# A causal convolution whose projections recompute the three tokens before each tile, in place of stored history columns

## The chip, the core and the metric

The kernel runs on one core of a Trainium2 chip. The metric is device time in microseconds for one execution, the median of three runs. One more execution was taken with the hardware profiler, and all rows below come from it.

## The reference, cut to what matters

One layer of a streaming encoder over 1024 tokens of 1024 features, in float32: a mixer (gated DeltaNet heads beside an RG-LRU), cross-attention into 256 memory tokens, a product-key expert layer (PEER) and a final RMSNorm. The part that the change touches is the mixer's input projection and the short convolution behind it:

```python
def causal_dwconv(x, w, b=None):
    s = x.shape[1]
    xp = jnp.pad(x, ((0, 0), (CONV_W - 1, 0), (0, 0)))
    y = sum(xp[:, j:j + s] * w[j] for j in range(CONV_W))
    return y if b is None else y + b
...
    proj = h @ w_in
    qkv, z, a_in, b_in, xr, gate = jnp.split(proj, offs, axis=-1)
    qkv = jax.nn.silu(causal_dwconv(qkv, conv_qkv_w))
    ...
    xr = causal_dwconv(xr, lru_conv_w, lru_conv_b)
```

`CONV_W` is 4, so each output token needs the projected columns of its own token and of the three before it. `h` is the RMS-normed input.

## The kernel before

The sequence is worked through in four passes of T = 256 tokens. A pass (`heads`) norms its 256 tokens, transposes them into `hT` (128 features on the partitions, 8 groups of features, 256 tokens), and then projects: `proj_T` loads one weight tile of 512 KB into one of three buffers `w`, and runs eight matmuls that add up 128 output channels x 256 tokens in a PSUM bank `pj`. A float32 matmul stands in the trace as two instructions of TensorE. Sixteen of these projections per pass feed a convolution: tiles 4 to 11 and 0 to 3 are q, k and v of the DeltaNet, tiles 12 to 15 are the LRU input, and four more (16 to 19, the LRU gate) and `wz` feed none. Pass 0 (tokens before `EARLY` = 256) runs its projections as three fp32r products of high and low parts (`Pair`, `mm3`) in place of float32.

`conv` (line 428) works on a buffer `cbuf` of 259 columns, of which there are two. VectorE copies the three columns that the pass before left in `hist` into columns 0 to 2 (line 431). ScalarE copies the 256 projected columns behind them (line 432). VectorE copies the last three back into `hist` for the next pass (line 433). ScalarE writes the newest tap into the output (line 434), and VectorE adds the three older taps from shifted windows of `cbuf` (line 436).

The passes form a chain: `delta` runs the DeltaNet recurrence of a pass in many small matmuls, and starts the next pass's `heads` from within. Beside it runs the stream `attended` (cross-attention, then PEER queries and top-16 searches, `UNITS` of 128 or 256 tokens). PEER's experts are computed in two ways. Tokens 256 to 767 go through a dense product over all experts (`dense`, with one-hot gate tables built by `gates` before it), TensorE's work of the second half. The other 512 tokens are gathered: each of 1024 steps reads 128 rows by an indirect DMA into `rb` (issued by GpSimd) and runs one VectorE instruction of 128x1024 on them. These steps are strewn over the whole kernel.

The order of all this is decided while the program is written. Each engine has a model clock (`Engine`): VectorE is charged 68 ns plus 1.04 ns per element, TensorE 1.67 ns per column of a float32 matmul. `together` always takes a stream whose time has come on TensorE's model clock, and `Paced.tick` puts in a gather step each 2.8 us (later 3.5 us) of TensorE's model time, if VectorE's model clock is less than `SLACK` = 8 us ahead of TensorE's:

```python
            while self.ns > self.pace and (not self.real or dve.at < self.at + SLACK and not late_row()):
                self.ns -= self.pace
                step()
```

In `dense` the steps that are left are spread evenly. Each engine executes its own queue in order.

Of the kernel before, what the change touches and what calls it, by code (L numbers as in the profile page):

```python
# [8 lines left out]
F = mybir.dt.float32  # L9
# [4 lines left out]
AF = mybir.ActivationFunctionType  # L14
# [3 lines left out]
D = 1024  # L18
S = 1024
T = 256  # L20
# [22 lines left out]
EARLY = T  # L43
# [6 lines left out]
def block_kernel(ctx: ExitStack, tc: tile.TileContext, a):  # L50
# [209 lines left out]
    def norm(X, nb, Y, junk):  # L260

        ss = small.tile([128, nb], F, name="n_ss")
        for b in range(nb):
            act.activation(junk, X[b], AF.Square, accum_out=ss[:, b:b + 1])
        dve.tensor_scalar(ss, ss, 1.0 / D, EPS, op0=OP.mult, op1=OP.add)
        rstd = rsqrt(ss, nb, "n_")
        for b in range(nb):
            act.activation(Y[b], X[b], AF.Copy, scale=rstd[:, b:b + 1])
        return rstd
# [15 lines left out]
    def low(i):  # L285

        return early[:, 2 * i:2 * i + 2, :].rearrange("p s (c t) -> p (s c) t", c=D // T)

    def transposed(hT, Y, nb, wcol):

        for c in range(8):
            if c:
                yield 0
            pt = bank("tp", 2)
            for b in range(nb):
                pe.transpose(pt[:, b * 128:(b + 1) * 128], Y[b][:, c * 128:(c + 1) * 128], identf)
            hi = hT.hi if isinstance(hT, Pair) else hT
            act.activation(hi[:, c, :], pt[:, :nb * 128], AF.Copy, scale=wcol[:, c:c + 1])
            if hi is not hT:
                dve.scalar_tensor_tensor(hT.lo[:, c, :], pt[:, :nb * 128], wcol[:, c:c + 1],  # L300
                                         hi[:, c, :].bitcast(F), op0=OP.mult, op1=OP.subtract)
# [122 lines left out]
    def heads(fp, P, prev, qkv):  # L424

        t0, ready = P.t0, P.ready

        def conv(ps, ti, w, out, bias=0.0):

            buf = fp.tile([128, T + 3], F, name="cbuf", bufs=CB)  # L430
            dve.tensor_copy(buf[:, 0:3], hist[:, ti, :])
            act.copy(buf[:, 3:3 + T], ps[:, :T])
            dve.tensor_copy(hist[:, ti, :], buf[:, T:T + 3])
            act.activation(out, ps[:, :T], AF.Identity, scale=w[:, 3:4], bias=bias)
            for j in range(3):
                dve.scalar_tensor_tensor(out, buf[:, j:j + T], w[:, j:j + 1], out, op0=OP.mult, op1=OP.add)

        def tmp():
            return fp.tile([128, T], F, name="cy", bufs=CB)

        while prev and "y" not in prev.ready:
            yield None
        pe.pace = PACES[t0 // T]
        hT = fp.tile([128, 8, T], F, name="hT", bufs=1)
        if prev:
            X = blocks_of(qkv[:, 4:12, :])
            norm(X, NB, X, hT[:, 0:D // T, :].rearrange("p c t -> p (c t)"))
            yield list(X)
        if t0 < EARLY:
            hT = Pair(hT, low(0), tmp)  # L450
        yield from transposed(hT, blocks_of(qkv[:, 4:12, :]), NB, wmixc)


        ps = bank("pj", 2)
        for c in range(8):
            if t0 < EARLY:
                mm3(ps[:8, :T], (wabh[:, c, :], wabl[:, c, :]), (hT.hi[:, c, :], hT.lo[:, c, :]), c == 0, c == 7)
            else:
                pe.matmul(ps[:8, :T], wab[:, c, :], hT[:, c, :], start=c == 0, stop=c == 7)
        abT = fp.tile([128, T], F, name="cth", bufs=1)[:8, :]  # L460
        act.copy(abT, ps[:8, :T])
        pt = bank("tp", 2)
        for b in range(NB):
            pe.transpose(pt[:, b * 8:(b + 1) * 8], abT[:, b * 128:(b + 1) * 128], identf[:8, :8])
        ab = small.tile([128, NB, 8], F, name="ab")
        act.copy(ab, pt[:, :NB * 8])
        if t0 == 0:
            constants()
        xg = small.tile([128, NB, 4], F, name="xg")
        dve.tensor_add(xg, ab[:, :, 0:4], dtb[:, None, :].to_broadcast([128, NB, 4]))  # L470
        spg = softplus(xg.rearrange("p a b -> p (a b)"), NB * 4, "spg").rearrange("p (a b) -> p a b", b=4)
        g = small.tile([128, NB, 4], F, name="g")
        dve.scalar_tensor_tensor(g, spg, -1.0, ealog[:, None, :].to_broadcast([128, NB, 4]),
                                 op0=OP.mult, op1=OP.mult)
        beta = small.tile([128, NB, 4], F, name="beta")
        act.activation(beta, ab[:, :, 4:8], AF.Tanh, scale=0.5)
        dve.tensor_scalar(beta, beta, 1.0, 0.5, op0=OP.add, op1=OP.mult)


        for j in (4, 5, 6, 7, 8, 9, 10, 11, 0, 1, 2, 3):  # L480
            while j == 0 and prev and not prev.finished():
                yield None
            ps = yield from proj_T("wA", j, hT, T)
            y = fp.tile([128, T], F, name="cy", bufs=CB)
            conv(ps, j, hcw[:, j, :], y)
            th = fp.tile([128, T], F, name="cth", bufs=1)
            act.activation(th, y, AF.Tanh)
            dve.scalar_tensor_tensor(qkv[:, j, :], th, 1.0, y, op0=OP.add, op1=OP.mult)

        zs = fp.tile([128, NB, 4, 128], F, name="zs", bufs=1)  # L490
        yl = fp.tile([128, 4, T], F, name="yl", bufs=1)
        P.g, P.beta, P.zs, P.yl = g, beta, zs, yl

        def side():

            for j in range(4):
                ps = yield from proj("wz", j, hT, NB)
                th = fp.tile([128, T], F, name="cth", bufs=1).rearrange("p (b m) -> p b m", b=NB)
                act.activation(th, ps, AF.Tanh, scale=0.5)
                dve.scalar_tensor_tensor(zs[:, :, j, :], th, 1.0, ps, op0=OP.add, op1=OP.mult)  # L500

            ready.add("z")


            for j in range(4):
                ps = yield from proj_T("wA", 12 + j, hT, T)
                xf = fp.tile([128, T], F, name="lxf", bufs=1)
                conv(ps, 12 + j, lconvw[:, j, :], xf, bias=lpar[:, 0, j:j + 1])
                pg = yield from proj_T("wA", 16 + j, hT, T)
                yield L_CONV  # L510
                ge = fp.tile([128, T], F, name="lge", bufs=1)
                act.activation(ge, pg[:, :T], AF.Gelu_apprx_tanh)
                pr = bank("pj")[:, :T]
                pe.matmul(pr, wga[:, j, :], xf, start=True, stop=True)
                px = bank("pj")[:, :T]
                pe.matmul(px, wgx[:, j, :], xf, start=True, stop=True)
                yield 0
                tx = fp.tile([128, T], F, name="ltx", bufs=1)
                act.activation(tx, px, AF.Tanh, scale=0.5, bias=hba[:, 1, j:j + 1])
                dve.scalar_tensor_tensor(tx, tx, 1.0, xf, op0=OP.add, op1=OP.mult)  # L520
                tr = fp.tile([128, T], F, name="ltr", bufs=1)
                act.activation(tr, pr, AF.Tanh, scale=0.5, bias=hba[:, 0, j:j + 1])


                rc = fp.tile([128, T], F, name="lrc", bufs=1)
                act.activation(rc, tr, AF.Exp, scale=nsp4[:, j:j + 1], bias=nsp4[:, j:j + 1])
                act.activation(tr, tr, AF.Tanh, scale=sp2[:, j:j + 1], bias=sp2[:, j:j + 1])
                act.activation(rc, rc, AF.Copy, scale=0.5, bias=0.5)
                nw = xf
                dve.scalar_tensor_tensor(nw, tr, 1.0, rc, op0=OP.add, op1=OP.mult)  # L530
                dve.scalar_tensor_tensor(rc, nw, 2.0, rc, op0=OP.subtract, op1=OP.mult)
                act.activation(tr, tr, AF.Sqrt)
                dve.tensor_mul(tr, tr, rc)
                dve.scalar_tensor_tensor(tx, tr, -1.0, tx, op0=OP.mult, op1=OP.mult)
                act.activation(rc, rc, AF.Copy, scale=-2.0, bias=-1.0)
                dve.tensor_tensor_scan(yl[:, j, :], rc, tx, lstate[:, j:j + 1], op0=OP.mult, op1=OP.add)
                dve.tensor_copy(lstate[:, j:j + 1], yl[:, j, T - 1:T])
                dve.tensor_mul(yl[:, j, :], yl[:, j, :], ge)
            ready.add("y")

        yield Stream(side(), RANK[2], SHARE[2])
# [724 lines left out]
    act.copy(wabh, wab)  # L1266
    dve.tensor_sub(wabl, wab, wabh.bitcast(F))
    norm_x(fp, qkv)
    hist = fc.tile([128, 16, 3], F, name="hist")
    dve.memset(hist, 0.0)  # L1270
    lstate = fc.tile([128, 4], F, name="lstate")
    dve.memset(lstate, 0.0)

# [119 lines left out]
```

## Time and profile before

| | us |
|---|---|
| median of three runs | 3198.26 |
| lowest and highest of them | 3195.79, 3198.62 |
| the profiled execution | 3195.01 |
| its span, first to last instruction | 3193.2 |

The span is what the rows below divide up; 1.8 us lie around it. Mean granted TensorE clock 0.971 of full speed. Over the span TensorE is busy 93% (its matmul ends are modelled and overlap, so this overstates it), VectorE 83%, ScalarE 40%, GpSimd 43%.

### The profile page before, as it was taken

The page shows a single profiled execution, that of the slowest core. Times are in us where ns is not written, and L with a number is a line of the kernel's source. Part 1 is how long each engine was busy: PE and PEld are TensorE (multiplying, and loading weights), DVE is VectorE, ACT ScalarE, POOL GpSimd, SP SyncE. Part 2 cuts the span into 40 slices and gives each one's busy share as a digit, 9 for nine tenths or more (in the row PEclk, how much of TensorE's full clock was granted, in tenths as well). Part 3 has the DMA queues.
Part 4 walks back from the last instruction along what each step waited for, and adds up shares of the span by engine and source line. Part 5 has one row for each costly group of instructions (what it writes and reads, how often), then busy time and mean ns, then how long its engine had stood idle before and what let it go on. Part 6 is the DMA issues. An engine that isn't in the chain of part 4 may idle for free.

```text
span 3193.2 us, 46214 instructions
## 1 busy us (share of the span) xinstructions
PE 2960.5 (93%) x16212; PEld 2535.3 (79%) x16212; DVE 2655.3 (83%) x5871; ACT 1278.3 (40%) x2630; POOL 1361.6 (43%) x1046
## 2 busy tenths in 40 slices
PE   6899899899999898888767999999999999999998
PEld 6889888888888788777656877777888878878886
DVE  7652577897786987998997999888889898889898
ACT  6844264256324531666476323222322222222222
POOL 0000023345332443343423665656565566666563
PEclk9999999999999999998878999999999999999999
DMA  5244768988787678898979899999999999999995
GB/s 175 93 146 146 233 243 315 324 303 308 270 288 272 239 278 314 292 323 285 308 242 318 323 341 337 346 348 343 359 355 351 352 335 339 350 345 353 351 341 212
DMA packets 321544, 941.63 MB, mean 295 GB/s; under 512 B 28912, under 2 KB 108832, under 8 KB 319264
## 3 DMA queue, kind: packets, MB, share of 16 engines
q0 software_dynamic: 148048, 538.04, 47.3%
q1 hardware_dynamic: 107216, 367.08, 31.3%
q10 hardware_dynamic: 66048, 33.56, 3.7%
q8 instruction: 128, 2.10, 0.3%
q14 instruction: 104, 0.85, 0.1%
HBM read 894.53 MB, written 44.04 MB: 294 GB/s over the span
## 4 chain that ended last, share of the span: by engine, by line
PE 33%; DVE 23%; issue 18%; POOL 10%; DMA 9%; ACT 6%; POOLq 0%; SPq 0%; DVEq 0%; ACTq 0%
PE pj L108 13%; POOL rb L1170 10%; DVE rb L83 8%; PE dh L108 7%; PE po L108 7%; PE gd L108 4%; DVE oh L83 3%; DMA rb<-in_v,idx 2%; DMA gd<-stage 2%; DVE i L83 1%; PE tp L113 1%; DMA w<-in_pwq 1%; ACT ohg L83 1%; DVE s L83 1%; DVE mr L83 1%
## 5 line engine op out<-in xcount | busy, mean ns | idle before, releaser
L1170 POOL DMA_INDIRECT rb<-in_u,idx x512 | 671.8, 1312 | 1113.9 <-DVE rb L83 433.8
L1170 POOL DMA_INDIRECT rb<-in_v,idx x512 | 680.7, 1330 | 678.2 <-DVE rb L83 472.8
L83 DVE SCALAR_TENSOR_TENSOR rb<-rb,ga 128x1024 f32<-128x1024 f32 x512 | 656.0, 1281 | 29.0 <-DMA rb<-in_v,idx 23.2
L83 DVE SCALAR_TENSOR_TENSOR rb<-rb 128x1024 f32<-128x1024 f32 x512 | 612.4, 1218 | 65.2 <-DMA rb<-in_u,idx 64.5
L108 PE MATMUL pj<-hT,w 128*128 128x256 f32 (+1 forms) x2880 | 586.0, 355 | 16.9 <-DMA w<-in_pwq 14.6
L108 PEld LDWEIGHTS pj<-hT,w 128*128 128x128 f32 x2880 | 486.2, 193 | 71.4 <-DMA w<-in_pwq 16.4
L83 ACT CAST uh<-ur 128x1024 fp32r<-128x1024 f32 x128 | 134.6, 1051 | 757.3 <-PE dh L108 714.5
L108 PE MATMUL dh<-hT_h,uh 128*128 128x512 f32 x1024 | 408.3, 399 | 8.0 <-ACT dg L83 7.3
L108 PE MATMUL po<-vh,dah 128*128 128x512 f32 x1024 | 405.2, 396 | 8.7 <-DVE acc L83 8.7
L108 PE MATMUL dh<-hT_h,ul 128*128 128x512 f32 x1024 | 407.2, 398 | 0.8 <-DVE ul L83 0.7
L108 PE MATMUL dh<-hT_l,uh 128*128 128x512 f32 x1024 | 407.3, 398 | 0.0
L108 PE MATMUL po<-vl,dah 128*128 128x512 f32 x1024 | 404.8, 395 | 0.0
L108 PE MATMUL po<-vh,dal 128*128 128x512 f32 x1024 | 404.6, 395 | 0.0
L108 PE MATMUL gd<-ohg,oh 128*128 128x128 f32 x1024 | 182.4, 334 | 81.7 <-ACT ohg L83 66.2
L108 PEld LDWEIGHTS gd<-ohg,oh 128*128 128x128 f32 x1024 | 165.2, 233 | 98.4 <-ACT ohg L83 91.3
L108 PEld LDWEIGHTS po<-vh,dah 128*128 128x128 f32 x1024 | 192.0, 187 | 60.7 <-DVE acc L83 14.2
L108 PEld LDWEIGHTS dh<-hT_h,uh 128*128 128x128 f32 x1024 | 193.8, 189 | 56.2 <-ACT dg L83 8.2
L108 PEld LDWEIGHTS dh<-hT_h,ul 128*128 128x128 f32 x1024 | 193.7, 189 | 48.7 <-DVE ul L83 1.7
L108 PEld LDWEIGHTS dh<-hT_l,uh 128*128 128x128 f32 x1024 | 194.0, 189 | 46.8
L108 PEld LDWEIGHTS po<-vl,dah 128*128 128x128 f32 x1024 | 192.1, 188 | 46.7
L108 PEld LDWEIGHTS po<-vh,dal 128*128 128x128 f32 x1024 | 192.0, 188 | 46.1
L83 DVE TENSOR_TENSOR ul<-ur,uh 128x1024 fp32r<-128x1024 f32 x128 | 155.6, 1222 | 58.7 <-ACT uh L83 58.2
(341 smaller groups left out, 4628.0 us busy)
## 6 DMA issues: line engine op xcount, KB each, us to landing
ur<-in_ut SPq DMA_DIRECT2D x128, 512.0 KB, 6.7
vr<-in_v SPq DMA_DIRECT2D x128, 512.0 KB, 6.4
w<-in_wA SPq DMA_DIRECT2D x80, 512.0 KB, 4.4
w<-in_pwq SPq DMA_DIRECT2D x80, 512.0 KB, 5.2
gd<-stage ACTq DMA_DIRECT2D x32, 1024.0 KB, 9.5
G<-gd SPq DMA_DIRECT2D x16, 2048.0 KB, 10.9
w<-in_wout SPq DMA_DIRECT2D x40, 512.0 KB, 4.3
w<-in_wq SPq DMA_DIRECT2D x40, 512.0 KB, 5.3
```

The costliest lines, as they stand in the source:

```text
L83: r = call(*args, **kw)
L108: self.engine.matmul(out, l, r, **kw)
L113: self.engine.transpose(out, i, ident)
L1170: pool.indirect_dma_start(out=t, out_offset=None, in_=a[ph], in_offset=bass.IndirectOffsetOnAxis(ap=B["idx"][:, k:k + 1], axis=0))
```

## The change

The input tile gets three more columns in front, `hTk`, and `hT` becomes a view of its last 256. At the end of a pass's transposes VectorE saves the last three normed token columns of all eight groups in `P.tail`; the next pass copies them into the first three columns of its `hTk`. In passes 1 to 3 the sixteen convolved projections run over 259 columns, so that the three columns in front are computed again and ScalarE moves all 259 into `cbuf` at once. In pass 0 the three are a memset. `hist` and both copies around it are gone. The gate and `wz` projections and the a/b product read `hT`, which now starts three columns into the tile.

```diff
-        def conv(ps, ti, w, out, bias=0.0):
+        def conv(ps, w, out, bias=0.0):
             buf = fp.tile([128, T + 3], F, name="cbuf", bufs=CB)
-            dve.tensor_copy(buf[:, 0:3], hist[:, ti, :])
-            act.copy(buf[:, 3:3 + T], ps[:, :T])
-            dve.tensor_copy(hist[:, ti, :], buf[:, T:T + 3])
-            act.activation(out, ps[:, :T], AF.Identity, scale=w[:, 3:4], bias=bias)
+            if not prev:
+                dve.memset(buf[:, 0:3], 0.0)
+            act.copy(buf[:, 3 - k:], ps[:, :T + k])
+            act.activation(out, ps[:, k:T + k], AF.Identity, scale=w[:, 3:4], bias=bias)
...
-        hT = fp.tile([128, 8, T], F, name="hT", bufs=1)
+        k = 3 if prev else 0
+        hTk = fp.tile([128, 8, T + 3], F, name="hT", bufs=1)
+        hT = hTk[:, :, 3:]
         if prev:
             X = blocks_of(qkv[:, 4:12, :])
-            norm(X, NB, X, hT[:, 0:D // T, :].rearrange("p c t -> p (c t)"))
+            norm(X, NB, X, hTk.rearrange("p c t -> p (c t)")[:, :D])
+            dve.tensor_copy(hTk[:, :, 0:3], prev.tail)
             yield list(X)
         if t0 < EARLY:
             hT = Pair(hT, low(0), tmp)
+        hk = hTk if prev else hT
         yield from transposed(hT, blocks_of(qkv[:, 4:12, :]), NB, wmixc)
+        P.tail = small.tile([128, 8, 3], F, name="tail")
+        if t0 < EARLY:
+            dve.tensor_add(P.tail, hT.hi[:, :, T - 3:].bitcast(F), hT.lo[:, :, T - 3:].bitcast(F))
+        else:
+            dve.tensor_copy(P.tail, hT[:, :, T - 3:])
...
-            ps = yield from proj_T("wA", j, hT, T)
+            ps = yield from proj_T("wA", j, hk, T + k)
...
-                ps = yield from proj_T("wA", 12 + j, hT, T)
+                ps = yield from proj_T("wA", 12 + j, hk, T + k)
...
-    hist = fc.tile([128, 16, 3], F, name="hist")
-    dve.memset(hist, 0.0)
```

## Rows read from the trace of the kernel before

PE is TensorE's matmuls, PEld its weight loads, DVE VectorE, ACT ScalarE, POOL GpSimd. Almost every row carries line 83 or 108, a helper that issues all instructions, so rows are told apart by the names of their tiles.

**Rows 1.** Windows: from:to and length, busy us of each engine (instructions), clock, DMA share, GB/s.
```profile
300.00:550.00 250.00, 231.08 (x1644) 210.80 (x1644) 164.10 (x606) 112.54 (x290) 48.48 (x44) 0.99 0.75 258
550.00:800.00 250.00, 232.92 (x1594) 213.80 (x1594) 215.94 (x660) 113.20 (x284) 103.65 (x91) 1.00 0.88 311
800.00:1060.00 260.00, 252.56 (x1638) 228.10 (x1637) 199.08 (x562) 101.17 (x249) 80.84 (x72) 1.00 0.78 273
1060.00:1300.00 240.00, 216.13 (x1411) 196.51 (x1411) 206.05 (x734) 75.50 (x181) 91.15 (x75) 0.96 0.80 284
1300.00:1735.00 435.00, 335.05 (x1885) 299.84 (x1884) 401.04 (x1257) 282.33 (x760) 168.38 (x131) 0.85 0.88 294
1735.00:3160.00 1425.00, 1412.69 (x6033) 1131.79 (x6032) 1273.12 (x1449) 405.33 (x452) 861.47 (x613) 1.00 0.93 343
```

**Rows 2.** Instructions of the tile `hist`: duration ns min/median/max, first and last start us.
```profile
L83 DVE COPY hist<-cbuf x64: 144/162/367, 33.4 to 1044.3; 128x3 f32<-128x3 f32 x64
```

**Rows 3.** Chain that ended last: start us, us, what (instructions merged).
```profile
765.93 3.46 PE pj L108 x16
...
1889.13 5.60 PE dh L108 x24
```

**Rows 4.** Waits from 1300 to 1735 us: total us, times, longest.
```profile
PE gd L108 <- ACT ohg L83: 66.2, 48, 7.0
ACT ohg L83 <- DVE oh L83: 53.2, 37, 8.9
```

**Rows 5.** Groups by line, VectorE, 1300 to 1735 us: count, busy us, mean ns, idle before.
```profile
L83 DVE SCALAR_TENSOR_TENSOR rb<-rb 128x1024 f32<-128x1024 f32 x110 | 132.4, 1214 | 2.7 <-DMA rb<-in_u,idx 2.7
...
L83 DVE SCALAR_TENSOR_TENSOR rb<-rb,ga 128x1024 f32<-128x1024 f32 x21 | 26.9, 1281 | 0.3
...
L83 DVE DVE_READ_ACCUMULATOR rb<-rb 128x1 f32 x110 | 8.6, 79 | 0.0
```

**Rows 6.** Groups by line over the whole span: the two copies around `hist`.
```profile
L83 DVE COPY cbuf<-hist 128x3 f32<-128x3 f32 x64 | 11.9, 187 | 0.6
...
L83 DVE COPY hist<-cbuf 128x3 f32<-128x3 f32 x64 | 11.0, 172 | 16.6 <-ACT cbuf L83 16.5
```

**Rows 7.** Timeline of VectorE in pass 3: start us, us, instruction, idle before it.
```profile
854.86 0.17 DVE L83 COPY hist<-cbuf 128x3 f32<-128x3 f32 x1 [0.40 <-ACT cbuf L83]
855.24 0.48 DVE L83 SCALAR_TENSOR_TENSOR cy<-cbuf,hcw,cy 128x256 f32<-128x256 f32 x1 [0.21 <-ACT cy L83]
...
859.76 0.22 DVE L83 COPY hist<-cbuf 128x3 f32<-128x3 f32 x1
```

**Rows 8.** Timeline of ScalarE in the same stretch.
```profile
854.73 0.48 ACT L83 ACTIVATE cy<-pj,hcw 128x256 f32<-128x256 f32 x1
...
859.07 0.48 ACT L83 ACTIVATE cy<-pj,hcw 128x256 f32<-128x256 f32 x1
```

**Rows 9.** TensorE's waits from 300 to 1060 us.
```profile
PE pj L108 <- DVE lxf L83: 5.8, 8, 2.9
...
PE tp L113 <- DVE qkv L83: 3.0, 2, 1.7
```

**Rows 10.** VectorE's waits from 300 to 1060 us, the longest in total.
```profile
DVE X L83 <- PE pj L108: 44.5, 25, 4.2
```

**Rows 11.** Timeline, first instructions of VectorE.
```profile
0.83 0.10 DVE L83 MEMSET hist<- 128x48 f32 x1 [0.83 <-PEq L1385]
```

**Rows 12.** Timeline of all engines at the start of pass 3.
```profile
830.77 0.47 ACT L83 ACTIVATE hT<-tp,c_wmixc 128x256 f32<-128x256 f32 x1 [0.42 <-PE tp L113]
...
834.94 0.17 DVE L83 TENSOR_TENSOR xg<-ab,dtb 128x8 f32<-128x8 f32 x1 [3.47 <-ACT ab L83]
```

**Rows 13.** Groups by line, ScalarE copies out of PSUM, shapes kept apart.
```profile
L83 ACT COPY cbuf<-pj 128x256 f32<-128x256 f32 x64 | 23.5, 367 | 43.4 <-PE pj L108 43.3
L83 ACT COPY pqT<-pj 128x256 f32<-128x256 f32 x56 | 20.6, 369 | 152.0 <-PE pj L108 152.0
...
L83 ACT COPY pqT<-pj 128x128 f32<-128x128 f32 x32 | 8.5, 266 | 62.2 <-PE pj L108 62.2
```

More of the change, by code (lines that the diff above doesn't have):

```diff
@@ L482, in heads @@
                 yield None
-            ps = yield from proj_T("wA", j, hT, T)
+            ps = yield from proj_T("wA", j, hk, T + k)
             y = fp.tile([128, T], F, name="cy", bufs=CB)
-            conv(ps, j, hcw[:, j, :], y)
+            conv(ps, hcw[:, j, :], y)
             th = fp.tile([128, T], F, name="cth", bufs=1)
@@ L505, in side @@
             for j in range(4):
-                ps = yield from proj_T("wA", 12 + j, hT, T)
+                ps = yield from proj_T("wA", 12 + j, hk, T + k)
                 xf = fp.tile([128, T], F, name="lxf", bufs=1)
-                conv(ps, 12 + j, lconvw[:, j, :], xf, bias=lpar[:, 0, j:j + 1])
+                conv(ps, lconvw[:, j, :], xf, bias=lpar[:, 0, j:j + 1])
                 pg = yield from proj_T("wA", 16 + j, hT, T)
```

## The prediction, on record before the result

> **What bounds the kernel now.** I read the windows first, cut where the work changes [rows 1]. The convolutions' copies all start between 33 and 1044 us [rows 2], so the change acts on the first third only. There the reader is to see TensorE busy for most of every stretch at nearly full clock: 231 of 250, 233 of 250 and 253 of 260 us, while VectorE is busy 66%, 86% and 77%. From 1300 to 1735 us it is the other way round: VectorE 401 of 435 us, TensorE 335 at a clock of 0.85. From 1735 to 3160 us TensorE is full again. The chain that ended last [rows 3] says the same in the dense part: 24 matmuls take 5.60 us, 233.3 ns each, and 6144 of them (128 expert tiles x 48) 1433 us. That length is fixed. The change can move the end only by moving the moment at which the dense part starts, so by what the front, some 1730 us, takes.
>
> Inside the front I asked which wait ends last. In the last stretch before the dense part TensorE waits 66.2 us for ScalarE's one-hot tiles, which wait 53.2 us for VectorE [rows 4]: VectorE sets that stretch, and 110 + 21 gather steps in it (132.4 + 26.9 us, and 79 ns behind each of the first kind [rows 5]) take 168 of its 401 us. In the passes it is TensorE's own queue.
>
> **The change part by part.**
>
> *Removed from VectorE.* 64 copies of 187 ns and 64 of 172 ns [rows 6]: 11.97 + 11.01 = 23.0 us, of which 48 x 0.359 = 17.2 us in passes 1 to 3, and one memset of 0.10 us [rows 11].
>
> *Added to VectorE.* In pass 0, 16 memsets of three columns, 0 to 0.10 us each by the memset of 48 columns [rows 11], I take 0.08: 1.3 us. Four saves of the tail and three copies of it, 24 elements in eight runs of three: no row has the shape, the nearest is the copy of three at 172 to 187 ns [rows 6], the bound above twice that. I take 0.18: 7 x 0.18 = 1.3 us. VectorE so loses 23.1 - 2.6 = 20.5 us of work.
>
> *The wait in front of the second copy.* VectorE stood 16.5 us in all waiting for ScalarE's copy into `cbuf` before it could save the history [rows 6]. This wait isn't gained. The next VectorE instruction needs ScalarE's newest-tap result, which ScalarE makes right behind that copy. The timelines of both engines in pass 3 show it [rows 7, 8]: the copy into `hist` ran from 854.86 to 855.03 us, the first tap began at 855.24, and ScalarE had ended its part at 854.73 + 0.48 = 855.21. Without the copy the tap begins at the same time. Where VectorE is late instead, as at 859.76 us, when ScalarE's part had ended at 859.07 + 0.48 = 859.55, the copies' time is really saved. So each convolution gives between 0 and 0.36 us.
>
> *What of it lies on the path.* In the passes TensorE waits for VectorE's convolution results in two groups [rows 9]: 5.8 us in 8 waits for the LRU input and 3.0 us in 2 for q, k, v. Each of the ten can shrink by at most 0.36 us: 0 to 3.6 us, I take the middle, 1.8 us. The rest of the 20.5 us goes into time in which VectorE waits for others anyway (44.5 us for projections to add to the residual alone [rows 10]). If that cover were gone, all of the passes' saving would show; that is the second case below.
>
> *Added to TensorE.* Eight float32 matmuls of 256 columns are 16 instructions in 3.46 us [rows 3], 216 ns each, 0.845 ns per column. Three columns more are 2.5 ns, over 16 projections x 3 passes x 16 instructions = 768: 1.95 us, on the engine that sets the passes, so I count it whole. Below, it could hide in waits (0); above, see the fourth case. Pass 0 has no extra columns.
>
> *ScalarE.* 369 ns for 256 columns and 266 for 128 [rows 13] are 0.8 ns per column: 48 x 3 x 0.8 = 0.1 us, on an engine that is busy 113, 113 and 101 us in those stretches [rows 1]. Nothing.
>
> *New waits.* The save of the tail stands in VectorE's queue behind the last transposed group. At the start of pass 3 that group is written at 831.24 us, and VectorE's next instruction of the pass, the first on a and b, waits 3.47 us, until 834.94 [rows 12]. The save fits into that gap; behind it only gather steps could be queued, and one of 1.29 us fits as well. If the gap were missing, VectorE would lose up to 3.5 us in each of three passes. The copy of the tail into the next `hTk` needs the square sums' pass over the same columns to be done, for which VectorE's square root in front of it has already waited; the two scalings on ScalarE and a transpose come between it and the first matmul that reads it. Nothing. Dependencies between passes don't change: the next pass already waits for the last projection of the one before.
>
> *Shifted operands.* `hT` now starts behind three columns of a row of 259, so projections, gate and a/b products read, and ScalarE writes, at odd offsets. The trace has such writes: the copy into `cbuf` begins at column 3 and takes 367 ns, the same shape to column 0 of `pqT` takes 369 [rows 13]. So it costs ScalarE nothing. Of TensorE's reads no row shows any; I take 0 and keep the other end as a case.
>
> [...]
>
> *The sum.* +1.95 - 1.8 + 0.1 = about +0.2 us. From the profiled execution's 3195.0 us that is 3195.2; the median of the runs is 3.2 us above that execution, so 3198.4 in its terms. A measurement of this kernel tells about 0.2%, 6.4 us, from no change.
>
> *What the sum leaves out.* The order itself is computed from the model clocks, and these change: VectorE is charged about 71 ns per small copy, so 128 + 1 - 16 - 7 = 106 fewer are 7.5 us less model work, and TensorE is charged 1.9 us more. From the first pass on, gather steps and streams may be taken in another order. Nothing in the trace prices this, but its size is bounded by the guard: 7.5 us of model work is 7 gather steps at 1.13 us, and a step really costs 1.21 + 0.08 = 1.29 us [rows 5], so some 9 us either way where VectorE sets the pace.
>
> **The rivals.**
>
> *Faster: VectorE's freed time reaches the path.* For it: VectorE is busy 216 of 250 us, 206 of 240 and 401 of 435 in three stretches [rows 1], so its backlog may hold TensorE more often than the ten waits show. Against it: those waits are small, and VectorE itself idles in between. If it holds, passes 1 to 3 give 17.2 less the 1.1 us of saves and copies, less TensorE's 1.95: 14 us, 3184. It decides where VectorE's queue is late at most of the 48 convolutions and stays so to the end of the front. The same side is reached if the new order does nine or more of the 131 steps before 1300 us instead of after.
>
> *Slower: more gather steps in the VectorE-bound stretch.* The guard sees 7.5 us less work on VectorE and lets up to 7 more steps through. In the dense part they would have been free (TensorE is the bound there); between 1300 and 1735 us each costs 1.29 us on the engine that sets the end: +9 us, with the 1.95 of TensorE +11, so 3209. It decides from five extra steps there. For it: 131 steps stood there before, though nothing but the pace asks for them. Against it: the pace counts TensorE's time, which hardly changes, and the copies are gone before 1050 us, so a modelled backlog can have evened out by 1300.
>
> *Slower: shifted reads hold TensorE.* If its reads at odd offsets were 5% slower, 768 + 192 (gate) + 48 (a/b) instructions of 216 ns would lose 10.8 ns each: 10.9 us, and with the 1.95 +13: 3211. For it there is only that no row excludes it; against it, ScalarE's shifted writes at no price.
>
> **How the numbers follow.** No measurable change 0.40; faster 0.34 (the freed time 0.18, a luckier order 0.16: the known direct effects on VectorE all point down); slower 0.26 (extra steps or an unluckier order 0.20, shifted reads 0.06). The forecast is that of the first, 3198; its own range is 3192 to 3205. To leave out no more than two in ten I reach to 3181 (the 14 us and 3 more) and 3212 (the +13 us).
>
> **What would show it.** In the changed kernel's trace: no copies of 128x3 around `cbuf` except 16 memsets; projections of 259 columns, about 2.5 ns longer per instruction in the chain (16 in 3.50 us in place of 3.46); VectorE busy some 20 us less before 1060 us; its wait for ScalarE moved to the first tap; the dense part still 1433 us, so that the whole difference is the moment at which it starts. The prediction is wrong if that moment shifts by more than 6 us. Then the count of steps between 1300 and 1735 us, and TensorE's waits for `lxf` and `qkv`, tell which case it was.

## The result and the profile after

| | median us | lowest to highest | runs | ratio to before, 95% interval |
|---|---|---|---|---|
| before | 3201.12 | 3195.79 to 3209.39 | 8 | |
| after | 3216.99 | 3203.97 to 3226.53 | 8 | 1.0051 [1.0034, 1.0067] |
| after, a second time beside other runs of before | 3220.18 | 3211.54 to 3229.62 | 12 | 1.0041 [1.0028, 1.0055] |

The kernel became about 0.46% slower (the mean of the two), some 15 us. That lies above the range on record. The profiled execution of after took 3217.02 us, that of before 3195.01 ([rows 1] come from it), the low end of its runs; of the 22 us between them some 6 are the spread of before.

The page's first part, kernel after: busy time, share and instructions of each engine.

```profile
span 3215.3 us, 46108 instructions
...
PE 2974.8 (93%) x16212; PEld 2542.2 (79%) x16212; DVE 2640.6 (82%) x5765; ACT 1280.5 (40%) x2629; POOL 1356.7 (42%) x1046
```

VectorE runs 106 instructions fewer, as counted ahead, and is 14.7 us less busy than the 2655.3 us of before. Its idle time (span less busy) rose from 537.9 to 574.7 us. Nothing of what it was spared came out at the end.

The windows of both kernels, cut at the same events: the a/b product that opens each of the four passes, the last LRU multiplication of pass 3, the first and the last one-hot tile `ohg`, the first and the last `po` matmul. Columns as in [rows 1]. First after:

```profile
16.50:194.90 178.40, 156.18 (x1187) 146.14 (x1188) 116.14 (x350) 118.77 (x261) 0.00 (x0) 0.95 0.37 124
194.90:538.20 343.30, 316.79 (x2264) 290.23 (x2264) 189.73 (x653) 155.92 (x395) 43.80 (x38) 0.97 0.62 210
538.20:842.10 303.90, 288.66 (x1952) 260.70 (x1952) 247.56 (x728) 133.46 (x334) 121.08 (x105) 0.99 0.85 301
842.10:1081.20 239.10, 229.67 (x1423) 205.27 (x1423) 180.98 (x490) 93.73 (x227) 71.44 (x66) 0.99 0.77 263
1081.20:1304.40 223.20, 202.02 (x1336) 185.72 (x1334) 187.83 (x676) 69.38 (x163) 82.68 (x70) 0.97 0.79 279
1304.40:1730.50 426.10, 331.71 (x1906) 294.89 (x1905) 401.85 (x1293) 276.81 (x761) 159.85 (x132) 0.87 0.88 293
1730.50:1760.20 29.70, 24.14 (x81) 18.70 (x81) 16.49 (x24) 14.40 (x19) 5.07 (x4) 0.76 0.94 357
1760.20:3200.50 1440.30, 1423.83 (x6073) 1139.99 (x6071) 1284.21 (x1476) 405.95 (x456) 865.18 (x614) 1.00 0.92 338
```

The same stages of before:

```profile
16.70:191.90 175.20, 154.68 (x1186) 144.18 (x1186) 118.02 (x366) 118.33 (x261) 0.00 (x0) 0.96 0.37 126
191.90:524.40 332.50, 311.05 (x2261) 286.03 (x2260) 188.98 (x667) 153.77 (x394) 41.12 (x37) 0.99 0.62 211
524.40:828.90 304.50, 285.29 (x1954) 259.22 (x1954) 255.92 (x777) 132.91 (x334) 122.36 (x109) 1.00 0.88 312
828.90:1061.10 232.20, 226.90 (x1415) 203.70 (x1415) 181.43 (x516) 91.96 (x226) 70.11 (x63) 1.00 0.77 265
1061.10:1294.90 233.80, 210.76 (x1383) 191.68 (x1382) 199.85 (x708) 71.64 (x169) 90.54 (x75) 0.96 0.80 282
1294.90:1715.30 420.40, 324.79 (x1863) 292.42 (x1864) 397.85 (x1268) 276.61 (x758) 164.76 (x129) 0.86 0.88 293
1715.30:1748.30 33.00, 25.00 (x80) 19.33 (x81) 18.72 (x29) 15.68 (x20) 6.60 (x6) 0.77 0.88 332
1748.30:3178.00 1429.70, 1420.23 (x6072) 1138.18 (x6071) 1278.22 (x1468) 405.14 (x454) 858.49 (x611) 1.00 0.92 339
```

Stage by stage the 22.1 us between the spans are +3.2, +10.8 (pass 1), -0.6, +6.9 (pass 3), -10.6, +5.7 (one-hot), -3.3, +10.6 (dense), and -0.6 at both ends. The loss isn't in one place. Its two largest pieces are in pass 1 and in the dense part, and in the dense part the change has no instruction at all. These are single executions: two of one program (`e1` and `e9` below) took 340.9 and 335.2 us for pass 1, at a mean clock of 0.97 and 0.99, so a piece of a few microseconds in the passes can be chance.

The groups of after that answer to [rows 6, 13], by line with shapes kept apart:

```profile
L108 PE MATMUL pj<-hT,w 128*128 128x259 f32 x768 | 177.3, 383 | 1.6 <-DMA w<-in_wA 1.4
...
L83 DVE SCALAR_TENSOR_TENSOR cy<-cbuf,hcw,cy 128x256 f32<-128x256 f32 x144 | 69.0, 480 | 24.8 <-ACT cy L83 22.9
...
L83 ACT COPY cbuf<-pj 128x259 f32<-128x259 f32 x48 | 17.8, 371 | 38.7 <-PE pj L108 38.3
```

ScalarE's and TensorE's direct costs are near what was worked out. The wait that stood in front of the second copy (16.5 us in [rows 6]) now stands in front of the first tap, 22.9 us in all. In before the taps themselves had waited for 2.7 us:

```profile
L83 DVE SCALAR_TENSOR_TENSOR cy<-cbuf,hcw,cy 128x256 f32<-128x256 f32 x144 | 69.1, 480 | 4.4 <-ACT cy L83 2.7
```

ScalarE's copy takes 371 ns. The saves and copies of the tail, by tile:

```profile
L83 DVE COPY hT<-tail x3: 175/175/309, 167.0 to 828.2; 128x24 f32<-128x24 f32 x3
L83 DVE COPY tail<-hT x3: 177/179/180, 199.7 to 844.5; 128x24 f32<-128x24 f32 x3
```

From one matmul instruction of a projection to the next the trace has a median of 216 ns for 256 columns in both kernels, whether the operand is shifted or not, and 219 ns for 259 columns.

TensorE's waits in pass 1 of after (195 to 540 us), the two longest: total us, times, longest.

```profile
PE pj L108 <- DMA w<-in_wo: 8.5, 4, 3.1
PE tp L113 <- ACT qkv L83: 4.4, 2, 4.0
```

The first of them in the same stretch of before (192 to 525 us):

```profile
PE pj L108 <- DMA w<-in_wo: 1.2, 2, 1.0
```

Where they stand is shown by the timeline of after (SPq is SyncE's issue of transfers):

```profile
505.41 3.01 SPq L83 DMA_DIRECT2D w<-in_wo  x3
...
512.50 5.32 PE L108 MATMUL pj<-w,oT 128*128 128x128 f32 x32 [3.13 <-DMA w<-in_wo]
516.07 2.11 SPq L83 DMA_DIRECT2D w<-in_wo  x2
...
522.65 1.62 PE L108 MATMUL pj<-w,oT 128*128 128x128 f32 x6 [2.60 <-DMA w<-in_wo]
...
534.26 0.69 PE L113 MATMUL tp<-identf,qkv 128*128 128x128 f32 x2 [4.02 <-ACT qkv L83]
```

At the end of pass 1 the output projection of the attention works through its weight tiles with little else between: 16 of its matmul instructions take 1.95 us, and a tile of 512 KB lands a median of 6.8 us after its issue (480 to 560 us). That three buffers then don't cover the loads is read from these rows; no run tests it by itself. The norm of the next pass then has nothing beside it. Windows of 10 us of the same place, columns as in [rows 1]:

```profile
510.00:520.00 10.00, 7.50 (x52) 7.38 (x52) 4.04 (x19) 3.19 (x13) 2.50 (x2) 0.83 1.02 401
520.00:530.00 10.00, 7.40 (x53) 7.38 (x52) 6.58 (x22) 1.11 (x2) 3.51 (x3) 0.83 0.78 264
530.00:540.00 10.00, 4.49 (x17) 2.10 (x15) 4.76 (x24) 6.13 (x10) 1.16 (x2) 0.64 0.75 214
540.00:550.00 10.00, 10.00 (x43) 5.32 (x42) 2.40 (x15) 3.20 (x11) 0.00 (x0) 0.85 0.26 100
```

TensorE is busy 7.5, 7.4 and 4.5 us of ten, and the granted clock falls to a mean of 0.83, 0.83 and 0.64: it is 0.50 from 513 to 515, from 523 to 525 and from 533 to 542 us, and 1.00 from 510 to 512, from 516 to 522 and from 526 to 532. None of this belongs to a convolution. It is other work standing beside other work. Before has such a place too, 40 us earlier, and a window as little busy at full clock:

```profile
470.00:480.00 10.00, 7.66 (x39) 7.05 (x40) 9.13 (x30) 5.33 (x12) 4.85 (x5) 0.66 0.80 249
510.00:520.00 10.00, 7.66 (x66) 7.33 (x66) 6.23 (x31) 2.31 (x4) 1.36 (x2) 1.00 0.81 290
```

TensorE's waits in the dense part, after:

```profile
PE po L108 <- DVE acc L83: 11.6, 11, 2.0
PE dh L108 <- DVE ul L83: 3.2, 2, 2.8
```

and before:

```profile
PE po L108 <- DVE acc L83: 8.7, 9, 1.8
PE dh L108 <- DVE ul L83: 0.7, 1, 0.7
```

Together they are 14.8 us in place of 9.4; with 1.7 us in two smaller waits that makes 7.1 of the 10.6 us by which the stage grew. VectorE is 6.0 us busier there.

### The profile page after: what moved, and what is told of

The parts are those of the page before. It is cut to its first block, busy times and chain, and to the rows that moved or that the text cites. A ratio compares the mean times of both kernels' runs of the same rounds, so it can differ in the third digit from the quotient of the medians.

```text
span 3215.3 us, 46108 instructions
## 1 busy us (share of the span) xinstructions
PE 2974.8 (93%) x16212; PEld 2542.2 (79%) x16212; DVE 2640.6 (82%) x5765; ACT 1280.5 (40%) x2629; POOL 1356.7 (42%) x1046
## 4 chain that ended last, share of the span: by engine, by line
PE 53%; DVE 21%; DMA 10%; issue 7%; ACT 5%; POOL 3%; SPq 0%; DVEq 0%; POOLq 0%; ACTq 0%
PE pj L108 16%; PE dh L108 16%; PE po L108 15%; DVE rb L83 7%; PE gd L108 4%; DVE oh L83 4%; POOL rb L1180 3%; DMA gd<-stage 2%; DMA rb<-in_v,idx 2%; PE tp L113 2%; DMA w<-in_wout 1%; DMA rb<-in_u,idx 1%; PE sc L108 1%; DVE i L83 1%; ACT L83 1%
## 5 line engine op out<-in xcount | busy, mean ns | idle before, releaser
L108 PE MATMUL pj<-hT,w 128*128 128x256 f32 (+2 forms) x2880 | 590.6, 355 | 8.6 <-DMA w<-in_pwq 3.9
## 6 DMA issues: line engine op xcount, KB each, us to landing
G<-gd SPq DMA_DIRECT2D x16, 2048.0 KB, 11.1
```

The costliest lines, as they stand in the source:

```text
L108: self.engine.matmul(out, l, r, **kw)
```

## The experiments

After and before differ in two things at once: in the operations, and in the order of all the rest, since the order is computed from model clocks that the operations are charged to. In the trace of before, VectorE's 4783 instructions, ScalarE's 2438 and SyncE's 717 (without the accumulator reads and loads of tables and match values) started in the order in which the program writes them down. VectorE's two queues have 4654 instructions in common, and the longest order that they share holds 3473 of them; for SyncE it is 685 of 717 (instructions told apart by operation, names of tiles, and turn among equals). **Theory A**: the order costs the time. **Theory B**: the operations cost it, by the projections' width, the shifted operands or a wait that moved. Each ratio below is to runs of before on the same chip. The expectations name absolute times that start from before's 3201 us; beside the experiments before measured 3204.7 to 3208.7 us, so the ratios are what is to be compared.

### Operations and order taken apart

`e1` and `e9` are one kernel, measured on two chips: the operations of after, with the model clocks charged as before. `charge` moves a model clock and issues nothing; `.engine` issues and doesn't charge; `h` stands in for the history tile. VectorE's queue then shares 4458 of 4654 with before in order; the other 4% stand elsewhere all the same and are counted with the operations. The core of the edit to after:

```diff
             if not prev:
-                dve.memset(buf[:, 0:3], 0.0)
-            act.copy(buf[:, 3 - k:], ps[:, :T + k])
+                dve.engine.memset(buf[:, 0:3], 0.0)
+            h = Seen("hist", 3 * ti, 3)
+            charge(dve, [buf[:, 0:3], h])
+            act.engine.copy(buf[:, 3 - k:], ps[:, :T + k])
+            charge(act, [buf[:, 3:3 + T], ps[:, :T]])
+            charge(dve, [h, buf[:, T:T + 3]])
...
-            dve.tensor_copy(hTk[:, :, 0:3], prev.tail)
+            dve.engine.tensor_copy(hTk[:, :, 0:3], prev.tail)
```

(and 256 columns charged for a matmul of 259). `e2` is the converse, the operations of before with the model clocks charged as after; 4565 of VectorE's 4654 are then in the order of after, and all of SyncE's:

```diff
-            dve.tensor_copy(buf[:, 0:3], hist[:, ti, :])
-            act.copy(buf[:, 3:3 + T], ps[:, :T])
-            dve.tensor_copy(hist[:, ti, :], buf[:, T:T + 3])
+            dve.engine.tensor_copy(buf[:, 0:3], hist[:, ti, :])
+            if not prev:
+                charge(dve, [buf[:, 0:3]])
+            act.engine.copy(buf[:, 3:3 + T], ps[:, :T])
+            charge(act, [buf[:, 3 - k:], ps[:, :T]], T + k)
+            dve.engine.tensor_copy(hist[:, ti, :], buf[:, T:T + 3])
...
```

Expected of `e1`: 

> The changed kernel's instructions (259 columns, shifted tile, no history copies), but the planner's model clocks are charged exactly as in the kernel before, so that streams and gather steps are taken in the order of before. Theory 'order' (the changed model charges gave another order of the streams, and that order costs the 16 us): 3195 to 3205 us, no difference to the kernel before. Theory 'direct' (the new instructions themselves cost it: wider projections, shifted reads, VectorE held at the first tap or at the save of the tail): 3211 to 3223 us, as the changed kernel.

Expected of `e2`: 

> The instructions of the kernel before (history copies and all), but the planner's clocks are charged as in the changed kernel, so that the order is that of the changed kernel. Theory 'order': 3211 to 3223 us, as the changed kernel. Theory 'direct': 3195 to 3205 us, as the kernel before.

Expected of `e9`: 

> The first experiment once more (the changed kernel's instructions in the planner's order of before), because its runs were spread over 25 us. If the parts add up (shift 0, wider projections +2.9, absence of the copies +1.0 us) it comes out at about +4 us, 1.0012; if the new instructions cost more together than alone, at +9 us as at first, 1.0028.

Expected of `e8`, the kernel after once more: 

> The changed kernel once more, beside the three above on the same chip: 1.0051 times before if the first measurement holds, within 0.0035.

Measured: `e1` 1.0028 [1.0012, 1.0045], `e9` 1.0019 [1.0004, 1.0033], `e2` 1.0027 [1.0012, 1.0043], `e8` 1.0041 [1.0028, 1.0055]; `e9` lies between its two forecasts. Neither theory holds alone: the operations cost about half of the loss, and the order the other half.

Where the order's half lies, `e2` shows, whose instructions are those of before. Its waits in pass 1:

```profile
PE pj L108 <- DMA w<-in_wo: 7.4, 5, 2.8
PE tp L113 <- ACT qkv L83: 4.4, 2, 4.0
```

and in the dense part:

```profile
PE po L108 <- DVE acc L83: 10.6, 7, 3.2
PE dh L108 <- DVE ul L83: 2.5, 3, 1.9
```

They are the waits of after. With the order of before the first of them is 1.2 us (before), 0.8 (`e1`), 2.4 (`e7`) and 4.3 (`e9`). In the three profiles with the order of after (after, `e8`, `e2`) pass 1 took 341 to 349 us, pass 3 239 to 241, and the dense part 1436 to 1440; in six with the order of before (before, `e5`, `e6`, `e7`, `e1`, `e9`) 332 to 341, 232 to 236 and 1425 to 1430. The stage from pass 3 to the one-hot tiles goes the other way, 223 to 225 us against 233 to 238. So pass 3, the stage behind it and the dense part follow the order, whichever operations run. Pass 1 leans the same way, but its two ranges touch.

### The operations, part by part

`e5` shifts the operands alone. By theory B they could cost a part of the 9 us by which `e1` was slower (1.0028):

```diff
-        hT = fp.tile([128, 8, T], F, name="hT", bufs=1)
+        hTk = fp.tile([128, 8, T + 3], F, name="hT", bufs=1)
+        hT = hTk[:, :, 3:]
...
```

Expected: 

> The kernel before, with the input tile of a pass 259 columns wide and used from its third column on, as in the changed kernel, and nothing else: 256 columns, history copies kept. Every engine's queue is in the same order as before. [...] Theory 'shift is free' (216 ns per instruction at either offset in the changed kernel's trace): 0, within 3 us of before.

Measured: 0.9998 [0.9983, 1.0013], with every queue in the order of before. The group of the projections in `e5`:

```profile
L108 PE MATMUL pj<-hT,w 128*128 128x256 f32 x2112 | 487.5, 381 | 11.9 <-DMA w<-in_pwq 9.8 <-ACT lxf L83 0.9 <-ACT cbuf L83 0.5
```

and in before:

```profile
L108 PE MATMUL pj<-hT,w 128*128 128x256 f32 x2112 | 488.2, 382 | 11.2 <-DMA w<-in_pwq 9.0 <-ACT lxf L83 0.9 <-DMA w<-in_wA 0.8
```

A shifted read costs nothing that can be seen.

`e6` is `e5` with the tail and the projections of 259 columns, while ScalarE copies 256 columns and VectorE keeps the history copies. `e7` takes the history copies away (it leaves the convolution's history out: all four taps read the newest window) and keeps 256 columns. In both the model clocks are charged as before.

```diff
e6
...
-            ps = yield from proj_T("wA", j, hT, T)
+            ps = yield from proj_T("wA", j, hk, T + k)
...
-            act.copy(buf[:, 3:3 + T], ps[:, :T])
+            act.engine.copy(buf[:, 3:3 + T], ps[:, k:T + k])
+            charge(act, [buf[:, 3:3 + T], ps[:, :T]])
...
e7
-            dve.tensor_copy(buf[:, 0:3], hist[:, ti, :])
+            h = Seen("hist", 3 * ti, 3)
+            charge(dve, [buf[:, 0:3], h])
...
-            dve.tensor_copy(hist[:, ti, :], buf[:, T:T + 3])
+            charge(dve, [h, buf[:, T:T + 3]])
...
-                dve.scalar_tensor_tensor(out, buf[:, j:j + T], w[:, j:j + 1], out, op0=OP.mult, op1=OP.add)
+                r = dve.engine.scalar_tensor_tensor(out, buf[:, 3:3 + T], w[:, j:j + 1], out, op0=OP.mult, op1=OP.add)
...
```

Expected of `e6`: 

> The shifted tile, the saved tail and projections of 259 columns in passes 1 to 3, but the history copies kept as well, in the planner's order of before. Theory 'wider projections': the 9 us show here, 3211 to 3218. Theory 'the copies' absence': only the 1.95 us of TensorE's extra columns, +1 to +4 us.

Expected of `e7`: 

> The kernel before without the two history copies, in the planner's order of before; the older taps read the newest window, so the convolution's history is left out of the computation. Theory 'wider projections': equal to before or up to 4 us faster. Theory 'the copies' absence' (without them VectorE stands at the first tap and the local order on ScalarE's and VectorE's queues changes: a tile's tanh goes ahead of the next tile's newest tap): slower by 5 to 9 us although 20 us of VectorE's work are gone.

Measured: `e6` 1.0009 [0.9992, 1.0025], `e7` 1.0003 [0.9991, 1.0016]. Neither theory of the expectations comes out: `e6` isn't 9 us slower, nor is `e7` slower by 5 to 9. Without the copies VectorE has 129 instructions fewer (the 128 copies and a memset) and is busy 2644.2 us in place of 2655.3, and the time doesn't fall. That is 11.1 us less, 86 ns for each, where the copies are listed with 172 and 187 ns: on VectorE the record of a short instruction overlaps its neighbour's, as in this stretch of before, where a copy of 0.42 us has begun 0.12 us ahead of the next tap:

```profile
860.28 0.42 DVE L83 COPY cbuf<-hist 128x3 f32<-128x3 f32 x1
860.40 1.00 DVE L83 SCALAR_TENSOR_TENSOR cy<-cbuf,hcw,cy 128x256 f32<-128x256 f32 x2
```

The wait stands in front of the first tap in `e7` as it does in after:

```profile
L452 DVE SCALAR_TENSOR_TENSOR cy<-cbuf,hcw,cy 128x256 f32<-128x256 f32 x144 | 69.2, 481 | 24.6 <-ACT cy L83 22.7
```

### Other orders

A single order could be good or bad luck. `HOP` is a constant of the planner (100); other values write other orders of the same instructions. With 110, before's VectorE queue shares 3148 of its 4654 with the order at 100, with 90 it is 3063, with 101 it is 3642 (counted as above; the 3240 of an expectation below is a shorter count).

```diff
-HOP, SLACK, WAIT = 100.0, 8000.0, 1000.0
+HOP, SLACK, WAIT = 110.0, 8000.0, 1000.0
```

Expected of before with 110: 

> The kernel before with one constant of the planner's model, HOP, the time from a result to its reader on another engine, at 110 ns in place of 100: not one instruction differs, only their order. Theory 'order' in its wide form (any new order moves the time by some 0.3 to 0.5%, either way): outside 3195 to 3207 us, in either direction, with even chances. Theory 'direct', or an order that seldom matters: 3195 to 3207 us.

Of after with 110: 

> The changed kernel with HOP at 110 ns in place of 100: the instructions of the changed kernel in one more order. Theory 'order': as likely near or under 3201 us as near 3217, so it need not be slow; 3195 to 3215 us. Theory 'direct': 3211 to 3223 us, the 16 us stay whatever the order.

Of before and after with 90: 

> The kernel before with HOP at 90 ns in place of 100, no instruction changed, another order. Theory 'even lottery' (a new order is as often faster as slower): below 1.000 with a chance of one half. Theory 'before stands at a good order' (it was kept among many, so nearly every other order is slower): 1.001 to 1.004.

 

> The changed kernel with HOP at 90 ns. Theory 'even lottery': between 0.998 and 1.006 of before. Theory 'before stands at a good order': 1.002 to 1.006, as the other orders plus the 4 us of the new instructions.

Of before with 101: 

> The kernel before with HOP at 101 ns in place of 100, the smallest nudge tried: about 3240 of VectorE's 4654 instructions stay in the same relative order. Theory 'even lottery': below 1.000 with a chance of one half. Theory 'before stands at a good order': 1.001 to 1.004.

The two crossed kernels (`e1`, `e2`) at 110: 

> The changed kernel's instructions in the order that the planner made for the kernel before at HOP 110 (1.0016 with the old instructions). Theory 'the instructions cost about 7 us in any order': 1.003 to 1.005. Theory 'the loss is the order': 1.001 to 1.0025.

 

> The instructions of the kernel before in the order that the planner made for the changed kernel at HOP 110 (1.0064 with the new instructions). Theory 'the changed charges lead to worse orders each time': 1.003 to 1.005. Theory 'the instructions': 1.0015 or less, as the other orders of the old instructions.

At 90: 

> The changed kernel's instructions in the order of the kernel before at HOP 90 (1.0010 with the old instructions). Theory 'the instructions cost about 7 us in any order': 1.0025 to 1.0045. Theory 'the loss is the order': 1.0005 to 1.002.

 

> The instructions of the kernel before in the order of the changed kernel at HOP 90 (1.0062 with the new instructions). Theory 'the changed charges lead to worse orders each time': 1.003 to 1.005. Theory 'the instructions': 1.0015 or less.

Measured, ratios with intervals; "order of before" and "of after" say whose charges wrote the order:

| `HOP` | old operations, order of before | new operations, order of before | old operations, order of after | new operations, order of after |
|---|---|---|---|---|
| 100 | 1 | 1.0028 [1.0012, 1.0045], 1.0019 [1.0004, 1.0033] | 1.0027 [1.0012, 1.0043] | 1.0051 [1.0034, 1.0067], 1.0041 [1.0028, 1.0055] |
| 110 | 1.0016 [1.0, 1.0032] | 1.0047 [1.0033, 1.0060] | 1.0046 [1.0033, 1.0059] | 1.0064 [1.0040, 1.0088] |
| 90 | 1.0010 [0.9996, 1.0024] | 1.0049 [1.0033, 1.0065] | 1.0031 [1.0020, 1.0042] | 1.0062 [1.0041, 1.0083] |
| 101 | 1.0008 [0.9995, 1.0021] | | | |

With the two values of a cell averaged, the operations add 0.24, 0.31 and 0.39% in the order of before and 0.19, 0.18 and 0.31% in that of after: a mean of 0.27%, 8.6 us. The order adds 0.27, 0.30 and 0.21% with the old operations and 0.22, 0.17 and 0.13% with the new: 0.22%, 7.0 us. All twelve differences have one sign, though each by itself is uncertain by about 0.2%. No entry of the table is below before. Part of the entries at 110 and 90 goes with a lower granted clock (last section). `e11` and `e15` lie just above every range that was named for them, `e12` between its two.

The order's loss has no one place over the three: at 110 (`e14` against `e3`) pass 2 and pass 3 grow by 12 and 24 us and the two stages behind them shrink by 15 and 19, where at 100 pass 1 and the dense part grew. The dense part grew by 11 us at 110 too, and at 90 (`e16` against `e10`) it shrank by 12.

### The parts once more, in another order

`e17` is `e6` and `e18` is `e7` (history left out again), both with `HOP` 110; VectorE's queues share 4568 and 4537 of 4654 with that of `e3`.

Expected of `e17`: 

> The kernel before with HOP 110, its 768 projections of passes 1 to 3 widened to 259 columns over shifted tiles (and the tails kept), while ScalarE copies the same 256 columns as before and VectorE still copies the history; the order is that of the HOP 110 kernel, but for the tail copies. HOP 110 alone measured 1.0016 and all the new operations in that order 1.0047 of before, so 0.31% (10 us) belongs to the operations. If the wider projections carry it: 1.0035 to 1.0047. If the absence of the history copies carries it (by what runs earlier on VectorE): 1.002 to 1.0025, the 1.9 us of wider matmuls and little else. If each carries a part: near 1.003.

Expected of `e18`: 

> The kernel before with HOP 110 and no history copies on VectorE, the older taps reading the window that the newest reads (so the convolution's history is left out); projections stay 256 columns wide, the order is that of the HOP 110 kernel. If the wider projections carry the 0.31% that the operations cost in that order: 1.0016 as HOP 110 alone, or less by what VectorE is spared. If the absence of the history copies carries it: near 1.004. If each carries a part: near 1.003.

Measured: `e17` 1.0028 [1.0017, 1.0038], `e18` 1.0013 [1.0001, 1.0024]. Against the 1.0016 of `e3` the wider projections are +0.12%, the missing copies -0.03%; at 100 it was +0.09 and +0.03%. So the copies' absence is worth nothing that can be seen, twice, and the width about 0.1%, 3.4 us, none of it outside the uncertainty by itself. The two together make 0.12 and 0.09%, where all the operations at once made 0.24 and 0.31%. The remaining 0.12 and 0.22%, 4 and 7 us, are no larger than the uncertainty of such a sum, so it isn't shown that anything remains. If it does, it belongs to what is in after and in neither part, the copy of 259 columns on ScalarE and the sixteen memsets, or to the parts acting together. That piece was not placed.

## Why the prediction was wrong

**The step that failed** is "What the sum leaves out". It saw that the order would be computed anew, bounded that by "some 9 us either way", and left it at zero in the forecast. Measured, it is +8.6 us at `HOP` 100 (0.27%) and +7.0 in the mean: inside the bound, at its edge, and more than the whole sum. The bound came from the wrong price, though: gather steps that change places "where VectorE sets the pace". What the runs show in its place is other neighbours for TensorE's work: waits for `w<-in_wo` of 8.5 us in place of 1.2 at the end of pass 1, a norm with nothing beside it, a lower clock around both (0.83, 0.83 and 0.64), and 5.4 us more waiting for VectorE in the dense part. Those are the places at `HOP` 100; with other orders most of the loss lies elsewhere. The lower clock is local: over whole runs after (`e8`) loses no more to the clock than before, 101.7 us against 102.3 (last section).

**The sum** of +0.2 us was mis-sized too: the operations measured +0.27%, 8.6 us.
- TensorE's term (+1.95) has its size: 219 against 216 ns on 768 instructions are 2.3 us. The kernels with the wider projections alone read +2.9 us (0.09%) and +3.8 (0.12%).
- VectorE's saving (20.5 us) was twice too large: with all new operations in the order of before it is busy 10.1 (`e1`) and 10.9 us (`e9`) less, in the order of after 13.7 (after against `e2`). The listed durations were added up, and they overlap. So a convolution frees some 0.17 us of VectorE's time, not 0.36.
- The gain of 1.8 us from ten shorter waits didn't show: +0.03 and -0.03% without the copies. At 0 to 3.6 us it was too small for these runs to refute. In after the waits themselves shrank, 5.8 to 2.0 us for `lxf` and 3.0 to 1.8 for `qkv` over 300 to 1060 us, and others grew; with the order of before `lxf` still has 4.5 us (`e1`, `e9`).
- The wait at the second copy was not gained, as said: 22.9 us stand at the first tap.
- The save of the tail, 177 to 180 ns, and ScalarE's 371 ns are what was taken. The save fitted into its gap: in passes 1 to 3 of after VectorE stands 13.8 us at it and 7.9 at the first instruction on a and b, 21.7 together, where `e2`, without it, stands 20.6 at the latter alone.
- Shifted operands cost nothing that can be seen, 0.9998 [0.9983, 1.0013]: the trace has 216 ns per instruction either way.
- The measured parts add up to 0.12 and 0.09%, and all operations at once measured 0.24 and 0.31%. Why the operations cost 8.6 us stays open.

**"That length is fixed"**, of the dense part, failed by 6 to 11 us: its 6144 matmuls are the same, but VectorE's work beside them is placed differently, and TensorE waits for it, 14.8 us in place of 9.4.

**The rivals.** The faster one (freed time reaches the path) is refuted by `e7` and `e18`: VectorE spared its 128 copies, nothing gained. Where the freed time went has no one place. The wait for the projections added to the residual, which was to cover it, grew from 44.5 us [rows 10] to

```profile
DVE X L83 <- PE pj L108: 53.6, 25, 5.3
```

in after (VectorE's waits, 300 to 1060 us), but in `e7`, `e1` and `e9`, whose VectorE was spared as much in the order of before, it is 47.7, 45.0 and 44.2. The slower one had the right sign by a wrong mechanism: it asked for five gather steps more between 1300 and 1735 us. There were 114 + 20 against the 110 + 21 of [rows 5], three more, 3.9 us by its price; the one-hot stage is 5.7 us longer. Shifted reads are ruled out: 0.9998 [0.9983, 1.0013] (`e5`) against the 10.9 us, 0.34%, by which that case had the reads slower.

**The chances** stood at 0.20 for an unluckier order or extra steps, against 0.16 for a luckier one: the two sides were taken as almost even, and a sum near zero was put between them. Whether the order of after is worse by a rule or by three draws of the same sign, these runs don't tell.

## What to carry to other kernels

In a kernel whose order is computed from modelled costs, every edit of a charged operation is two changes, one of operations and one of order, and here the second cost about as much as the first: measure the edit with the old charges kept, and the old operations with the new charges, before either is judged. Three nudges of a constant that changes no instruction gave +0.08, +0.10 and +0.16%, none a gain and none by itself clear of no change; whether the order of before is a favourable draw, three runs don't show. Work taken from an engine that waits for others anyway was worth nothing here (+0.03 and -0.03%), and what it frees is less than the listed durations of the instructions that go (86 ns each, listed with 172 and 187). The columns added to the engine that sets the passes measured +2.9 and +3.8 us, near the 2.3 us of their matmuls, though neither is clear of no change.

## What the runs showed of the hardware

Runs of one kernel spread more than the three runs shown at first let expect: the 125 runs of before beside the experiments lie between 3194.6 and 3220.4 us, with a standard deviation of 5.0 us. Part of that is the granted clock: its mean over a run goes from 0.965 to 0.972, and the time of a run goes up by 0.56 us with each microsecond of (time x (1 - clock)), correlation 0.59, about a third of the spread's variance. The loss of after is not that: the mean of this product is 101.7 us for after (`e8`) and 102.3 for before beside it, and for `e2` 99.1 against 103.0. In other orders a part of the difference is. With `HOP` 110 in the order of before the product is 110.6 (`e3`), 119.2 (`e13`), 112.6 (`e17`) and 116.5 us (`e18`), against 103.0, 102.8, 104.5 and 104.5 for before beside them; at the 0.56 above that is an estimate of 4 to 9 us, of whole differences of 5, 15, 9 and 4 us. With 90 it is 105.8 (`e10`) and 109.1 (`e11`) against 99.2. Whether the order lowers the clock there, or the clock falls for another reason, no run shows.

Waits of 3.13, 2.60 and 4.02 us within 25 us stood beside a granted clock of 0.83, 0.83 and 0.64, so these short waits came with a slower TensorE around them. It isn't so each time: the two windows of before above, both with TensorE busy 7.66 us of ten, have a clock of 0.66 and of 1.00.

Short instructions on VectorE cost less than they are listed with: 129 of them taken away freed 86 ns each, where the two kinds of copy have means of 172 and 187 ns.
